# The triangular substitution of a hybrid encoder block's time mixer, on VectorE instead of GpSimd

## The chip, the cores and the metric

The kernel runs on one core of a Trainium2 chip. The metric is the device time of one execution in microseconds (us). Times quoted per run are those of whole executions; times of stages are counted from the first instruction of one profiled execution.

## The reference

The reference is one encoder block on `x` of 256 tokens by 2048 columns, all in float32: a projection, two mixers side by side, an output projection with layer norm, and a SwiGLU feed-forward with layer norm.

```python
proj = jnp.einsum('bsd,dc->bsc', x, w_in[l])
y_fourier = _fourier_mixer(proj[..., F_OFF:R_OFF])        # 512 columns, FFT over tokens and group
y_rwkv = _rwkv7_bidir(proj[..., R_OFF:], ...)             # 24 heads of 64, both directions
mix = jnp.einsum('bsc,cd->bsd', jnp.concatenate([y_fourier, y_rwkv], -1), w_out[l])
h = _layernorm(ALPHA * x + mix, ln1_g[l], ln1_b[l])
ff = jax.nn.silu(h @ w_ffn_gate[l]) * (h @ w_ffn_up[l])
x = _layernorm(ALPHA * h + ff @ w_ffn_down[l], ln2_g[l], ln2_b[l])
```

The bidirectional time mixer carries, for each head and direction, a 64 by 64 state over the tokens:

```python
sa = jnp.einsum('bhij,bhj->bhi', state, a_t)
state = (state * w_t[:, :, None, :] + sa[..., None] * b_t[:, :, None, :]
         + v_t[..., None] * k_t[:, :, None, :])
y_t = jnp.einsum('bhij,bhj->bhi', state, r_t)
```

## The kernel before

The kernel has two parts. The first holds the projection, both mixers, the output projection, the first norm and the start of the feed-forward; the second holds the rest. A float32 weight is split into a rounded part `hi` (ScalarE) and a remainder `lo` (VectorE, or GpSimd for every second half in the projections), and TensorE multiplies with both. `weights` (line 362) loads a block of 512 KB into one of three `raw` buffers and makes two halves in rings of six `hi` and six `lo`.

The time mixer doesn't walk over the tokens one at a time. The 24 heads are 12 pairs, two heads on the 128 partitions, and a loop runs over six double pairs, each with 4 chunks of 64 tokens and both directions. Its steps are:

- `prepare` (line 516), for each pair: projections of `k` and `r` with a token shift, the decays (`e`, `f` by two scans), the normed key `kx`, and the operands `ar` and `xb`. The receptance products are lines 574 to 576: `r` times `f`, once per head, 64 partitions by 512 elements. Masked score products `w` end the step.
- `extract` (line 627), for each pair: the 16 by 16 diagonal blocks of the chunks' triangular matrices go out to DRAM by 16 small copies of SyncE, and come back as one copy into `mt`, one block per partition row.
- `substitute` (line 647), for each double pair: it inverts the 16 by 16 blocks by forward substitution. In step s of 15 a product (into `tmp`) and an addition (into `tt`) take column s of `mt` off the rows below it, for up to 8 columns and both pairs. `tt` then goes to DRAM by one copy of SyncE, comes back into `eb` by 16, and VectorE transposes it into `et`.
- `invert` (line 669): TensorE and small copies build the 64 by 64 inverses `ti` from the blocks.
- `recur` (line 721), for the double pair before: the four chunks in turn (`sv`, `bg`, `v1s`), then the group norm, the bonus and the gate. The result goes to DRAM as `mix`, and later comes back to be split into `xT` for the output projection.

The order in which each engine issues is not written by hand. `Program` collects all operations with what they depend on. `cost` (line 145) gives each an estimate in nanoseconds, `schedule` (line 238) places them with a list scheduler on five engines, and `flush` (line 303) takes the shortest of 49 trial schedules (`TRIES`, line 337) and issues in its order. Operations inside `pr.fused()` are one unit there: their estimates are summed, and nothing of the same engine is issued between them. The estimate for a VectorE operation is line 172:

```python
return 69 + (0.52 if half else 1.04) * n + 60 * ptrs + (110 if part else 0)
```

Before the change the 30 operations of `substitute` are single units on GpSimd, so others of GpSimd can be issued between them.

Of the kernel before, what the change touches and what calls it, by code (L numbers as in the profile page):

```python
# [13 lines left out]
OP = mybir.AluOpType  # L14
# [37 lines left out]
def view(t, off, dims, parts=None):  # L52

    base = t if parts is None else t[parts[0]:parts[1]]
    return bass.AP(tensor=base.tensor, offset=base.offset + off, ap=[list(base.ap[0])] + [list(d) for d in dims])
# [12 lines left out]
class Program:  # L68
# [76 lines left out]
    def cost(self, eng, method, outs, ins, k, args):  # L145
        n = max(self.count(x) for x in outs + ins)
        psum = any("PSUM" in str(x.tensor._space) for x in outs + ins if hasattr(x.tensor, "_space"))
        ptrs = sum(1 for x in ins if self.count(x) == 1) if n > 1 else 0
        kw_op, part = k.get("op"), outs[0].ap[0][1] < 128
        if eng == "pe":  # L150
            n, m = self.count(outs[0]), self.count(ins[0])
            if ins[0].dtype == F32R:
                return max(107, n * 0.455)
            if method == "transpose":
                return 109 if m == 128 and ins[0].ap[0][1] == 128 else 56 if ins[0].ap[0][1] == 128 else 30
            side = 0.5 if ins[0].ap[0][1] == 64 or m == 64 else 1.0
            return max(m, n) * 4 / 2.4 * side + 3 if m != 32 else 15
        if eng == "act":
            return 54 + 0.833 * n + 93 * ptrs + (40 if not psum else 0) + (100 if part and not ptrs else 0)
        if eng == "pool":  # L160
            if kw_op == OP.pow:
                return 1250
            if method == "tensor_tensor":
                return 290 + 2.1 * n
            return (40 if method == "memset" else 147) + (0.9 if method == "memset" else 2.15) * n
        if eng == "sp":
            size = 4 * self.count(outs[0]) * list(outs[0].ap)[0][1]
            return max(330 if size < 16384 else 500, size / 360)
        if method == "reciprocal":
            return 65 + 6.5 * n  # L170
        half = method in ("tensor_copy", "tensor_scalar") and not psum
        return 69 + (0.52 if half else 1.04) * n + 60 * ptrs + (110 if part else 0)
# [6 lines left out]
    def add(self, queue, method, args, kw):  # L179
# [29 lines left out]
        if op < len(self.ops):  # L209
# [3 lines left out]
            o["banks"] |= banks  # L213
            return
        self.ops.append(dict(q=queue, calls=[(method, args, kw)], preds=list(preds), cost=cost, banks=banks,
                             bias=self.bias, rows=ins[0].ap[0][1] / 128 if eng == "pe" else 0,
                             e=["act", "dve", "pool", "pe", "sp"].index(eng), kind=kind))
# [115 lines left out]
EXCL = (1, [[259, 2], [65, 4], [1, 64]])  # L333
# [6 lines left out]
def body(ctx, tc, i, out):  # L340
    nc = tc.nc
    pr = Program(nc)
    act, dve, pool, pe, sp = pr.act, pr.dve, pr.pool, pr.pe, pr.sp
# [61 lines left out]
    with pr.ahead(AHEAD):  # L405
        for q in range(4):
            for j in range(2):
                n, k = 2 * q + j, slice(4 * q + 2 * j, 4 * q + 2 * j + 2)
# [7 lines left out]
                if j == 0:  # L416
                    parts = []
# [51 lines left out]
    for j, tl in enumerate((T_W, T_A)):  # L469
        t = lora[:, 2 + j, :]  # L470
# [3 lines left out]
    for j, tl in enumerate((T_G0, T_G1)):  # L474
        t = lora[:, j, :]
# [40 lines left out]
    def prepare(p, dec):  # L516
# [16 lines left out]
        e, f = R["e"].next(), R["f"].next()  # L533
# [30 lines left out]
        ar, xb = R["ar"].next(), R["xb"].next()  # L564
# [8 lines left out]
        shifted(T_R + p, r)  # L573
        for h, (a0, a1) in enumerate(HEAD):
            rb = r[a0:a1].rearrange("p (c t) -> p c t", t=64)[:, None].to_broadcast([64, 2, 4, 64])
            dve.tensor_tensor(ar[a0:a1, :, :, 1 + h, :], rb, view(f, *EXCL, parts=(a0, a1)), op=OP.mult)
        pool.tensor_tensor(bs, kd[:, 0, :], kd[:, 1, :], op=OP.add)
        dve.scalar_tensor_tensor(bs, bs, col(V_RK, p), r, op0=OP.mult, op1=OP.mult)

# [67 lines left out]
    def substitute(P, mt):  # L647

        msp = ms[P % 2]
        tt, tmp, e, et = (R[n].next() for n in ("tt", "tmp", "eb", "et"))  # L650
        act.copy(tt, eye2[:, None].to_broadcast([128, 2, 8, 16]))
        for s in range(15):
            m, t = min(8, s + 1), 15 - s
            x = tmp[:, 0:2 * m * t].rearrange("p (n j t) -> p n j t", n=2, t=t)
            pool.tensor_tensor(x, mt[:, :, None, s + 1:16, s].to_broadcast([128, 2, m, t]),
                               tt[:, :, 0:m, s:s + 1].to_broadcast([128, 2, m, t]), op=OP.mult)
            pool.tensor_tensor(tt[:, :, 0:m, s + 1:16], tt[:, :, 0:m, s + 1:16], x, op=OP.add)
        with pr.ahead(AHEAD):
            sp.dma_start(out=msp.rearrange("(n p) x -> p n x", n=2), in_=tt.rearrange("p n m t -> p n (m t)"))
            for j in range(2):  # L660
                for n, (h, b, a) in enumerate(quads):
                    for k in range(2):
                        r = a + 16 * k
                        sp.dma_start(out=e[r:r + 16, 8 * j:8 * j + 8, 16 * k:16 * k + 16],
                                     in_=msp[j * 128 + r:j * 128 + r + 16].rearrange("(c u) (m t) -> (u m) c t", u=2, t=16))
        dve.transpose(et.rearrange("p c t -> p (c t)"), e.rearrange("p c t -> p (c t)"))
        return (e, et), (et, e)
# [184 lines left out]
    for P in range(NPAIR // 2 + 1):  # L852
        if P < NPAIR // 2:
            dec, mt = R["dec"].next(), R["mt"].next()
            sts = []
            for n in range(2):
                sts.append(prepare(2 * P + n, dec[:, n]))
                if P == 1 and n == 0:
                    fourier_in()
                extract(2 * P + n, sts[n], mt)  # L860
                tokens(sts[n])
                sts[n]["v"] = R["v"].next()
                shifted(T_V + 2 * P + n, sts[n]["v"])
            diag = substitute(P, mt)
        if P:
            recur(P - 1, *last)
        if P < NPAIR // 2:
            sv = R["sv"].next()
            for n in range(2):
                values(2 * P + n, sts[n], sv)  # L870
            last = sts, invert(sts, diag), sv, dec
# [49 lines left out]
    for n, k in enumerate(2 * kp + j for kp in ORDER for j in range(2)):  # L921
        m = loads[n % 3]
# [96 lines left out]
    for f in range(FT):  # L1019
# [3 lines left out]
        parts = []  # L1023
# [102 lines left out]
```

## Time and profile before

| | |
|---|---|
| median of 3 runs | 1441.82 us (1440.95 to 1443.12) |
| profiled execution | 1441.34 us |
| its span, first to last instruction | 1439.5 us |
| mean granted TensorE clock, share of full | 0.968 |
| TensorE matmul busy | 1344.1 us, 93% of the span |
| VectorE busy | 852.4 us, 59% |
| ScalarE busy | 704.3 us, 49% |
| GpSimd busy | 398.2 us, 28% |

In the trace PE is TensorE, DVE is VectorE, ACT is ScalarE, POOL is GpSimd and SP is SyncE, whose DMA queue is SPq. Every operation goes through one helper, so all carry its line, 316; they are told apart by the names of what they write and read (`out<-in`, buffer numbers left out). The banks `nar` and `ch` share one name, `ch`. A time in square brackets is how long the engine stood idle before an instruction, with what released it. The mixer and the output projection take about the first 640 us of the span, the feed-forward the rest.

### The profile page before, as it was taken

What the parts mean: (1) busy time and instruction counts of PE and PEld (TensorE: products, weight loads), DVE (VectorE), ACT (ScalarE), POOL (GpSimd) and SP (SyncE); (2) the same over time, 40 slices, a digit from 0 to 9 for tenths busy, and PEclk for the clock granted to TensorE, in tenths of its full rate; (3) what the DMA queues carried; (4) which work ended last, traced back from release to release, by engine and by line L of the source; (5) the groups of instructions that cost most, each with busy time, mean ns of one, the idle gap of its engine ahead of it and who ended that gap; (6) DMA issues with size and microseconds to landing.
All of it is one profiled execution on the core that took longest, in us unless ns stands there. A gap on an engine that the chain in (4) does not pass through costs nothing.

```text
span 1439.5 us, 30790 instructions
## 1 busy us (share of the span) xinstructions
PE 1344.1 (93%) x12132; PEld 1172.2 (81%) x12132; DVE 852.4 (59%) x1427; ACT 704.3 (49%) x1367; POOL 398.2 (28%) x540
## 2 busy tenths in 40 slices
PE   6889899898979888989999999999999999999996
PEld 6888778887878776667888888888888888888896
DVE  4665367576655655556655555555555555555556
ACT  5545445445454543434555555555555554444442
POOL 3548437484744714002211111111111110000002
PEclk9999899899999989999999999999999999999999
DMA  7444423323242346443575555555555555555553
GB/s 243 134 131 133 149 87 113 85 87 99 76 150 74 105 131 192 139 160 131 176 238 187 190 190 184 186 188 190 190 184 186 187 191 190 190 191 192 191 187 132
DMA packets 102696, 228.77 MB, mean 159 GB/s; under 512 B 37528, under 2 KB 48280, under 8 KB 101912
## 3 DMA queue, kind: packets, MB, share of 16 engines
q1 hardware_dynamic: 102552, 226.82, 48.1%
q8 instruction: 95, 1.56, 0.4%
q14 instruction: 49, 0.40, 0.1%
HBM read 220.47 MB, written 6.29 MB: 158 GB/s over the span
## 4 chain that ended last, share of the span: by engine, by line
PE 51%; DVE 0%; DVEq 0%; issue 0%
PE ch L316 19%; PE mm L316 14%; PE sc L316 12%; PE yb L316 6%; DVE w L316 0%; DVE lrs L316 0%; DVEq L1122 0%; DVE lst L316 0%; DVE lmv L316 0%
## 5 line engine op out<-in xcount | busy, mean ns | idle before, releaser
L316 DVE TENSOR_TENSOR lo<-raw,hi 128x512 fp32r<-128x512 f32 x676 | 495.3, 737 | 382.7 <-ACT hi L316 358.5
L316 ACT CAST hi<-raw 128x512 fp32r<-128x512 f32 x760 | 465.7, 620 | 477.6 <-PE mm L316 123.7
L316 PE MATMUL mm<-xT,hi 128*128 128x256 f32 (+1 forms) x1776 | 414.4, 320 | 13.3 <-ACT hi L316 6.4
L316 PEld LDWEIGHTS mm<-xT,hi 128*128 128x128 f32 x1776 | 300.3, 199 | 35.3 <-issue 7.7
L316 PE MATMUL mm<-xT,lo 128*128 128x256 f32 (+1 forms) x1072 | 305.9, 293 | 2.6 <-DVE lo L316 1.7
L316 PEld LDWEIGHTS mm<-xT,lo 128*128 128x128 f32 x1072 | 210.7, 198 | 9.9 <-DVE lo L316 3.4
L316 PE MATMUL ch<-xT,hi 128*128 128x512 f32 x528 | 185.2, 397 | 0.0
L316 POOL TENSOR_TENSOR lo<-raw,hi 128x512 fp32r<-128x512 f32 x84 | 115.0, 1372 | 143.9 <-ACT hi L316 106.9
L316 POOL TENSOR_TENSOR fe<-fe,fe 128x256 f32<-128x256 f32 x44 | 32.7, 745 | 405.7 <-DVE fe L316 385.0
L316 PE MATMUL ch<-xT,lo 128*128 128x256 f32 x528 | 142.6, 281 | 0.0
L316 PE MATMUL sc<-xT,hi 128*128 128x512 f32 x352 | 121.9, 397 | 0.0
L316 PEld LDWEIGHTS ch<-xT,hi 128*128 128x128 f32 x528 | 96.9, 188 | 19.9
L316 PEld LDWEIGHTS ch<-xT,lo 128*128 128x128 f32 x528 | 99.6, 189 | 4.4
L316 PE MATMUL sc<-xT,lo 128*128 128x256 f32 x352 | 93.3, 280 | 0.0
L316 PE MATMUL ch<-hi,h 128*128 128x512 f32 x264 | 88.7, 390 | 0.0
L316 POOL TENSOR_TENSOR lrs<-lrs,mhalf 128x1 f32<-128x1 f32 x4 | 3.9, 972 | 290.5 <-DVE lrs L316 290.5
L316 PEld LDWEIGHTS sc<-xT,hi 128*128 128x128 f32 x352 | 63.9, 188 | 13.1
L316 PE MATMUL mm<-hi,h 128*128 128x512 f32 (+1 forms) x248 | 73.5, 359 | 0.0
L316 PEld LDWEIGHTS sc<-xT,lo 128*128 128x128 f32 x352 | 66.4, 189 | 2.9
L316 PE MATMUL yb<-xT,hi 128*128 128x512 f32 x176 | 63.7, 396 | 0.0
L316 PEld LDWEIGHTS ch<-hi,h 128*128 128x128 f32 x264 | 49.6, 188 | 10.7
L316 POOL TENSOR_TENSOR tmp<-mt,tt 128x96 f32<-128x96 f32 (+13 forms) x90 | 49.2, 547 | 19.2 <-DMA mt<-md 15.4
(214 smaller groups left out, 2058.5 us busy)
## 6 DMA issues: line engine op xcount, KB each, us to landing
raw<-in_w_gu_dram SPq DMA_DIRECT2D x176, 512.0 KB, 3.2
raw<-in_w_down_dram SPq DMA_DIRECT2D x88, 512.0 KB, 3.2
raw<-in_w_in_dram SPq DMA_DIRECT2D x84, 512.0 KB, 3.6
raw<-in_w_out_dram SPq DMA_DIRECT2D x32, 512.0 KB, 3.5
up<-in_lora_up_dram SPq DMA_DIRECT2D x12, 256.0 KB, 5.9
raw<-in_xT_dram SPq DMA_DIRECT2D x8, 256.0 KB, 4.9
raw<-in_w_in_dram SPq DMA_DIRECT2D x8, 256.0 KB
w<-in_x_dram SPq DMA_DIRECT2D x2, 1024.0 KB, 6.5
```

What stands on the lines that cost most here:

```text
L316: getattr(o["q"].engine, method)(*args, **kw)
```

## The change

`substitute` issues its 30 operations on VectorE, inside `pr.fused()`, so that they are one unit of the schedule. The receptance product of the second head of each pair goes to GpSimd; that of the first stays on VectorE. Five estimates of the planner change: a float32 matmul's cost per column, that of a matmul with 32 rows, a GpSimd `tensor_copy` (a formula of its own), the fixed part of a GpSimd `tensor_tensor`, and a small DMA issue of SyncE. Since the schedule is made from the estimates, the order of all engines' instructions in the first part can change, and that of the second as well.

```diff
--- before.py
+++ after.py
@@ -154,18 +154,20 @@
             if method == "transpose":
                 return 109 if m == 128 and ins[0].ap[0][1] == 128 else 56 if ins[0].ap[0][1] == 128 else 30
             side = 0.5 if ins[0].ap[0][1] == 64 or m == 64 else 1.0
-            return max(m, n) * 4 / 2.4 * side + 3 if m != 32 else 15
+            return max(m, n) * 4.5 / 2.4 * side + 3 if m != 32 else 31
         if eng == "act":
             return 54 + 0.833 * n + 93 * ptrs + (40 if not psum else 0) + (100 if part and not ptrs else 0)
         if eng == "pool":
+            if method == "tensor_copy":
+                return 147 + 0.85 * n
             if kw_op == OP.pow:
                 return 1250
             if method == "tensor_tensor":
-                return 290 + 2.1 * n
+                return 160 + 2.1 * n
             return (40 if method == "memset" else 147) + (0.9 if method == "memset" else 2.15) * n
         if eng == "sp":
             size = 4 * self.count(outs[0]) * list(outs[0].ap)[0][1]
-            return max(330 if size < 16384 else 500, size / 360)
+            return max(450 if size < 16384 else 500, size / 360)
         if method == "reciprocal":
             return 65 + 6.5 * n
         half = method in ("tensor_copy", "tensor_scalar") and not psum
@@ -573,7 +575,7 @@
         shifted(T_R + p, r)
         for h, (a0, a1) in enumerate(HEAD):
             rb = r[a0:a1].rearrange("p (c t) -> p c t", t=64)[:, None].to_broadcast([64, 2, 4, 64])
-            dve.tensor_tensor(ar[a0:a1, :, :, 1 + h, :], rb, view(f, *EXCL, parts=(a0, a1)), op=OP.mult)
+            (dve if h == 0 else pool).tensor_tensor(ar[a0:a1, :, :, 1 + h, :], rb, view(f, *EXCL, parts=(a0, a1)), op=OP.mult)
         pool.tensor_tensor(bs, kd[:, 0, :], kd[:, 1, :], op=OP.add)
         dve.scalar_tensor_tensor(bs, bs, col(V_RK, p), r, op0=OP.mult, op1=OP.mult)
 
@@ -649,12 +651,13 @@
         msp = ms[P % 2]
         tt, tmp, e, et = (R[n].next() for n in ("tt", "tmp", "eb", "et"))
         act.copy(tt, eye2[:, None].to_broadcast([128, 2, 8, 16]))
-        for s in range(15):
-            m, t = min(8, s + 1), 15 - s
-            x = tmp[:, 0:2 * m * t].rearrange("p (n j t) -> p n j t", n=2, t=t)
-            pool.tensor_tensor(x, mt[:, :, None, s + 1:16, s].to_broadcast([128, 2, m, t]),
-                               tt[:, :, 0:m, s:s + 1].to_broadcast([128, 2, m, t]), op=OP.mult)
-            pool.tensor_tensor(tt[:, :, 0:m, s + 1:16], tt[:, :, 0:m, s + 1:16], x, op=OP.add)
+        with pr.fused():
+            for s in range(15):
+                m, t = min(8, s + 1), 15 - s
+                x = tmp[:, 0:2 * m * t].rearrange("p (n j t) -> p n j t", n=2, t=t)
+                dve.tensor_tensor(x, mt[:, :, None, s + 1:16, s].to_broadcast([128, 2, m, t]),
+                                  tt[:, :, 0:m, s:s + 1].to_broadcast([128, 2, m, t]), op=OP.mult)
+                dve.tensor_tensor(tt[:, :, 0:m, s + 1:16], tt[:, :, 0:m, s + 1:16], x, op=OP.add)
         with pr.ahead(AHEAD):
             sp.dma_start(out=msp.rearrange("(n p) x -> p n x", n=2), in_=tt.rearrange("p n m t -> p n (m t)"))
             for j in range(2):
```

## Rows read from the trace of the kernel before

**Rows 1.** Page, busy time, share of the span and instructions of each engine

```profile
PE 1344.1 (93%) x12132; PEld 1172.2 (81%) x12132; DVE 852.4 (59%) x1427; ACT 704.3 (49%) x1367; POOL 398.2 (28%) x540
```

**Rows 2.** Busy time (instructions) of PE, PEld, DVE, ACT, POOL; clock; DMA; GB/s

```profile
0.00:640.00 640.00, 560.07 (x7863) 496.10 (x7864) 384.18 (x714) 300.84 (x625) 309.19 (x436) 0.94 0.40 126
```

**Rows 3.** Waits of TensorE, 0 to 640 us: total us, times, longest

```profile
PE ch L316 <- issue: 19.2, 10, 3.5
PE sc L316 <- DVE xb L316: 8.9, 5, 2.6
PE ch L316 <- DVE et L316: 7.3, 3, 4.1
...
PE mm L316 <- ACT xT L316: 5.0, 2, 4.8
...
PE sc L316 <- DVE ar L316: 2.2, 4, 1.0
...
PE mm L316 <- DVE lo L316: 1.3, 3, 0.9
```

**Rows 4.** Timeline of GpSimd, last substitution: start, us, instruction

```profile
535.75 0.25 POOL L316 TENSOR_TENSOR tmp<-mt,tt 128x30 f32<-128x30 f32 x1 [6.54 <-DMA mt<-md]
...
555.97 0.70 POOL L316 TENSOR_TENSOR tt<-tt,tmp 128x16 f32<-128x16 f32 x1
```

**Rows 5.** Timeline of VectorE and TensorE, end of the mixer

```profile
569.33 0.71 DVE L316 STREAM_TRANSPOSE et<-eb 128x512 f32<-128x512 f32 x1 [4.27 <-DMA mix<-yn]
...
625.74 0.80 PE L316 MATMUL mm<-hi,xT 128*128 128x512 f32 x1 [4.80 <-ACT xT L316]
...
626.76 1.05 PE L316 MATMUL mm<-hi,xT 128*128 128x512 f32 x2
...
631.67 0.63 PE L316 MATMUL sc<-hi,xT 128*128 128x512 f32 x2
```

**Rows 6.** Groups of GpSimd by names: count | busy us, mean ns | idle before

```profile
L316 POOL TENSOR_TENSOR tmp<-mt,tt 128x96 f32<-128x96 f32 (+13 forms) x90 | 49.2, 547 | 19.2 <-DMA mt<-md 15.4
L316 POOL TENSOR_TENSOR tt<-tt,tmp 128x96 f32<-128x96 f32 (+13 forms) x90 | 40.6, 451 | 3.5
```

**Rows 7.** Timeline of VectorE, products of two SBUF operands, and a dependent operation

```profile
303.75 0.42 DVE L316 TENSOR_TENSOR r<-pp 128x256 f32<-128x256 f32 x1
304.21 0.48 DVE L316 SCALAR_TENSOR_TENSOR r<-mm,omm,r 128x256 f32<-128x256 f32 x1
...
344.44 0.68 DVE L316 TENSOR_TENSOR ar<-r,f 64x512 f32<-64x512 f32 x1
```

**Rows 8.** Busy time, last substitution to the late xT (columns as in 2)

```profile
535.75:625.74 89.99, 77.16 (x1117) 58.72 (x1116) 46.01 (x122) 36.97 (x80) 24.65 (x40) 0.97 0.52 167
```

**Rows 9.** Timeline of TensorE, the first of its three waits for et

```profile
166.80 0.45 PE L316 MATMUL ch<-et,w 32*32 32x32 f32 x32 [4.14 <-DVE et L316]
```

**Rows 10.** Timeline of VectorE, 455.6 us on, beside the fifth substitution's start

```profile
455.77 0.43 DVE L316 COPY sv<-ch 64x256 f32<-64x256 f32 x1 [2.01 <-ACT sv L316]
457.00 0.42 DVE L316 TENSOR_TENSOR k<-pp 128x256 f32<-128x256 f32 x1 [0.80 <-ACT pp L316]
```

**Rows 11.** Busy time summed over the stretches of the first five substitutions

```profile
sum 175.68, PE 164.84 PEld 148.67 DVE 121.51 ACT 83.53 POOL 152.96; mean PE 32.97 PEld 29.73 DVE 24.30 ACT 16.71 POOL 30.59
```

**Rows 12.** Timelines of GpSimd and VectorE from 46 us

```profile
46.25 1.30 POOL L316 TENSOR_TENSOR lo<-raw,hi 128x512 fp32r<-128x512 f32 x1 [1.33 <-ACT hi L316]
...
46.58 1.25 DVE L316 TENSOR_TENSOR k<-pp 128x256 f32<-128x256 f32 x1 [1.11 <-ACT pp L316]
```

**Rows 13.** Groups by shape: receptance products, and GpSimd's product of 512 elements

```profile
L316 DVE TENSOR_TENSOR ar<-r,f 64x512 f32<-64x512 f32 x24 | 23.6, 984 | 1.7 <-ACT f L316 1.0
...
L316 POOL TENSOR_TENSOR xb<-th,e 128x512 f32<-128x512 f32 x12 | 15.0, 1253 | 0.1
```

**Rows 14.** SyncE's issues into eb (ns min/median/max), and GpSimd's copy of 512

```profile
L316 SPq DMA_DIRECT2D eb<-ms x96: 302/429/1860, 155.8 to 566.0; - x96
...
L316 POOL COPY w<-ar 64x512 f32<-64x512 f32 x12 | 7.1, 613 | 61.9 <-PE ch L316 61.9
```

## The prediction

> **What bounds the kernel now.** I began with the page's busy shares: TensorE is busy for 93% of the span, VectorE for 59%, GpSimd for 28% [rows 1]. The reader is to see that no vector engine is near its limit, so a vector operation matters only through what TensorE waits for. The edited code runs in the mixer, so I then took the stretch of its 640 us: TensorE is busy 560.1 us there, VectorE 384.2, GpSimd 309.2, with a granted clock of 0.94 [rows 2]. TensorE's 79.9 us of idle time there is nearly all that the change can win. The waits of TensorE in that stretch say what it is made of [rows 3]: 19.2 us is time that no engine released, 8.9 us waits for VectorE's `xb`, 7.3 us for its `et` (the transpose behind the substitution), 5.0 us for ScalarE's `xT`, 2.2 us for `ar`, and only 1.3 us for a `lo` half of a weight.
>
> Next I followed one substitution through the timeline. The last one starts on GpSimd at 535.75 us and its last addition ends at 556.67 [rows 4]. Behind it come the copies through DRAM, the transpose at 569.33, the last inversion and recurrence, and then TensorE stands still for 4.80 us, up to 625.74, because the last mixer columns arrive late as `xT`; after the stop its matmuls are spaced at the lower clock level (two take 1.05 us, five us later 0.63) [rows 5]. So at the end of the mixer the chain through the substitution does set the time; before it, TensorE has other products to run.
>
> **The substitution moves.** It is 30 dependent operations, six times. On GpSimd they are busy 49.2 + 40.6 = 89.8 us [rows 6], 15.0 us each time; with other GpSimd work let in between them, the last takes 20.9 us and the other five 32 to 39. VectorE has no such row, so I price it by its rows [rows 7]: a product of 256 elements takes 0.42 us, one of 512 takes 0.68, which is 0.16 us fixed and 1.02 ns an element; a dependent operation starts 0.04 us after the one before it ends. The 15 steps hold 2 x min(8, s+1) x (15-s) elements, 1192 in sum, twice. So 30 x 0.20 + 2384 x 0.00102 = **8.4 us** a substitution, 50 us in all. VectorE would stand at 384 + 50 - 12 (below) = 422 of 640 us, 66%: still no bound. The same 17 SyncE issues follow each substitution as before, and wait for VectorE instead of GpSimd; behind them on SyncE wait weight loads and the next pair's gather.
>
> *At the end of the mixer* the chain gets 20.9 - 8.4 = 12.5 us shorter. TensorE is idle 12.8 us between the start of that substitution and its 4.80 us stop's end [rows 8], and 12 matmuls behind the stop lose some 0.2 us each, 2.4 us. Bounds: nothing (if something else is late next, the last weight loads being nearest) and -12.5. I take the stop and its slow matmuls, **-7.2 us**, as the other idle pieces there belong to the inversion's own steps. What is late next is the inversion, whose buffers the recurrence before it must leave first.
>
> *In the five earlier double pairs* TensorE waited for `et` three times, 7.3 us in sum [rows 3], 4.14 of it the first time [rows 9]. Elsewhere matmuls cover the substitution's 32 to 39 us, and a shorter one is worth nothing. Bounds 0 and -7.3; the transpose waits for 17 issues of SyncE as well as for the substitution, so I take a little over half, **-4 us**.
>
> *The run holds VectorE.* One unbroken run means that what was let in between GpSimd's steps now queues behind 8.4 us: at one such landing these are the recurrence's `sv`, then `k` of the next pair [rows 10], and `lo` halves; ScalarE and TensorE wait for the first, TensorE and SyncE's buffer release for the last. The five stretches in which GpSimd ran them leave VectorE 175.7 - 121.5 = 54.2 us idle [rows 11], more than the 42 us of five runs. Bounds: nothing, if they fill that idle time, and 42 us, if TensorE waits them out. Weight halves are made ahead (1.3 us of waits in 640), which covers the `lo`; if that stock is gone, each run costs up to its length. I take 1 us a run, **+5 us**, near the lower end by the small waits in rows 3.
>
> The low end of the run's own length, 8.4 us, holds only while GpSimd lies still. A VectorE product of 256 elements that began at 46.58, inside GpSimd's split of 46.25 to 47.55, took 1.25 us and not 0.42: it ended 0.28 us after the split did [rows 12]. GpSimd's share without the substitutions is (309.2 - 89.8 + 15) / 640 = 37%, so the run may stretch to 8.4 / 0.63 = 13.3 us. The Trainium skill, "SBUF — State Buffer", section "SBUF: two separate sides", states this as a rule: an operation of VectorE with two SBUF inputs and one of GpSimd that reads SBUF take a shared port pair in turn, each for a whole instruction. The trace agrees, by that 1.25 us. By the row alone I keep 8.4 to 13.3 us as bounds; taken at its full strength, the rule gives the slower rival below, 1449, where the sum here gives 1434.
>
> **The receptance product** of the second head goes to GpSimd, 12 times. On VectorE each takes 0.98 us in the mean [rows 13], 0.68 undisturbed [rows 7]: -12 x 0.98 = -11.8 us of VectorE time. On GpSimd the nearest product of as many elements takes 1.25 us: +15 us. The two heads' products would run in turn by rows 12, so the path to the score matmuls grows by 1.25 - 0.68 = 0.6 us a pair, 7 us if all lay on TensorE's path; it waits 2.2 us for `ar` now. Behind it on GpSimd waits `bs`, which has time. Bounds -2 and +7; **+1 us**.
>
> **The estimates** change only the order in which each engine issues. A 16-row gather or scatter issue takes 0.43 us [rows 14]; the plan says 0.33 now and 0.45 after, and 48 of them per double pair make 4.8 us that SyncE falls behind. A copy of 512 elements on GpSimd takes 0.61 us [rows 14], planned at 1.25 and then 0.58. These two move towards the rows. The plan prices the new VectorE run at 30 x 0.069 + 2384 x 0.00104 = 4.55 us, 3.9 below my price: that moves away. A new order can win at most what TensorE waits on small steps, nearest the 8.9 us for `xb`, or lose as much. I take a quarter, **-2 us**.
>
> The sum is -7.2 - 4 + 5 + 1 - 2 = -7.2 us. The profiled execution took 1441.34 us (span 1439.5 and 1.84 around it), 0.48 under the median of the runs, 1441.82; so **1434.1 us**, said as 1434.
>
> **Rivals.** *Slower: the run is locked apart and TensorE waits.* With GpSimd's splits in turn with its steps a run takes 13.3 us, 8.7 over its plan; whatever VectorE was to make for the recurrence and the next pair comes that much late, and TensorE, which issues in order, stops at the first of them with all products behind it. At 4 us for each of five runs, +20 and not +5: 1434 + 15 = 1449 us. It decides from 2.4 us a run on, where gains of 12.2 are used up. For it: rows 10 and 12, and VectorE is 69% busy in those stretches. Against it: the 54 us of idle time, and few waits for `lo`. It has a chance of 0.27; the Trainium skill's rule named above is this mechanism, and its own part is the lock.
>
> *No difference.* The planner may place the run late, or the last chain's gain may turn into a wait for the inversion or for loads; TensorE's products then take their old time and the terms cancel: 1441 us, chance 0.16. For it: TensorE was busy through most of the substitutions (164.8 of 175.7 us [rows 11]).
>
> *A larger gain.* All 12.5 us of the last chain and all 7.3 us of the waits for `et` go, and the runs hide: 1441.3 - 19.8 = 1421.5 us, chance 0.12. Against it: inversion steps whose waits have no releaser.
>
> **How the numbers follow.** The forecast of 1434 has a chance of 0.45; its own range is 1428 to 1438 (all of the `et` waits and a little more of the last chain, or runs of 2 us). The range of 1421 to 1452 takes in the larger gain and the slower rival with 4.6 us a run. A measurement tells 0.2% (2.9 us) from nothing: faster 0.45 + 0.12 = 0.57, same 0.16, slower 0.27.
>
> **What would show it.** Right: the 30 operations on VectorE in 8 to 10 us, GpSimd near 325 us in all, no 4.80 us stop of TensorE before `xT`, and waits for `et` under 4 us. The lock: VectorE steps of 1 us and more among rows of 0.2 to 0.3, a run of 13 us, and longer waits of TensorE for `sv`, `k`, `xb` or `lo`. The forecast is wrong if the last substitution does not start sooner after its gather, or if the mixer's TensorE idle time grows although its end is free.

## The result and the profile after

The changed kernel takes 1462.01 us in the median of 3 runs (1458.36 to 1464.48), against 1441.82 before: a ratio of 1.0136, 95% interval 1.0100 to 1.0173. It is slower, and outside the forecast range. The profiled execution took 1464.48 us, its span 1462.7.

First the page's busy shares:

```profile
PE 1343.0 (92%) x12132; PEld 1176.9 (80%) x12132; DVE 911.0 (62%) x1595; ACT 704.6 (48%) x1367; POOL 337.4 (23%) x372
```

And the mixer's window (columns as in [rows 2]); what was 640 us long now takes 663:

```profile
0.00:663.00 663.00, 562.06 (x7884) 502.77 (x7885) 444.04 (x886) 302.70 (x628) 247.82 (x268) 0.92 0.40 123
```

Against [rows 2], GpSimd has 61 us less, VectorE 60 us more. TensorE's busy time grew by only 2 us, its idle time from 79.9 to 100.9: the 23 us are idle TensorE time, nearly all. No engine became the bound; VectorE is busy 67% of the mixer.

The waits of TensorE in the stretch (total us, times, longest) say for whom:

```profile
PE ch L318 <- DVE yn L318: 28.4, 5, 7.5
PE ch L318 <- issue: 20.5, 11, 3.2
PE sc L318 <- DVE xb L318: 7.0, 3, 4.4
PE mm L318 <- DVE lo L318: 6.7, 1, 6.7
...
PE ch L318 <- DVE et L318: 0.8, 1, 0.8
PE mm L318 <- ACT xT L318: 0.6, 3, 0.2
```

In [rows 3] `et` stood at 7.3 and `xT` at 5.0: both are nearly gone, as forecast. In their place stands VectorE's `yn`, the group norm's result, which had cost little in the kernel before:

```profile
PE ch L316 <- DVE yn L316: 3.4, 4, 1.0
```

TensorE's timeline has one stop behind each of the six runs:

```profile
129.36 0.58 PE L318 MATMUL mm<-xT,lo 128*128 128x256 f32 x1 [6.70 <-DVE lo L318]
...
223.00 1.11 PE L318 MATMUL ch<-ident,yn 128*128 128x128 f32 x4 [6.97 <-DVE yn L318]
...
309.87 0.47 PE L318 MATMUL ch<-ident,yn 128*128 128x128 f32 x1 [7.39 <-DVE yn L318]
...
398.64 1.12 PE L318 MATMUL ch<-ident,yn 128*128 128x128 f32 x4 [7.47 <-DVE yn L318]
...
485.56 1.11 PE L318 MATMUL ch<-ident,yn 128*128 128x128 f32 x4 [6.40 <-DVE yn L318]
...
574.94 1.98 PE L318 MATMUL sc<-f,ta 128*65 128x129 f32 x8 [4.41 <-DVE xb L318]
```

Together 39.3 us. What stands ahead of the second, first on VectorE's timeline (start, length, instruction):

```profile
209.64 0.69 DVE L318 TENSOR_TENSOR yn<-yb,mv 128x512 f32<-128x512 f32 x1
210.24 1.22 DVE L318 TENSOR_TENSOR k<-pp 128x256 f32<-128x256 f32 x1
211.38 0.19 DVE L318 TENSOR_TENSOR tmp<-mt,tt 128x30 f32<-128x30 f32 x1
...
212.98 1.35 DVE L318 TENSOR_TENSOR tmp<-mt,tt 128x96 f32<-128x96 f32 x1
214.36 0.26 DVE L318 TENSOR_TENSOR tt<-tt,tmp 128x96 f32<-128x96 f32 x1
...
215.73 1.31 DVE L318 TENSOR_TENSOR tt<-tt,tmp 128x120 f32<-128x120 f32 x1
...
222.17 0.19 DVE L318 TENSOR_TENSOR tt<-tt,tmp 128x16 f32<-128x16 f32 x1
222.26 0.68 DVE L318 TENSOR_TENSOR yn<-yn,rs 128x512 f32<-128x512 f32 x1
```

and beside it on GpSimd's:

```profile
211.12 1.83 POOL L318 TENSOR_TENSOR rs<-rs,mhalf 128x8 f32<-128x8 f32 x1
212.92 1.29 POOL L318 TENSOR_TENSOR lo<-raw,hi 128x512 fp32r<-128x512 f32 x1
...
215.63 1.27 POOL L318 TENSOR_TENSOR lo<-raw,hi 128x512 fp32r<-128x512 f32 x1 [1.43 <-ACT hi L318]
```

The group norm takes the mean off on VectorE, lets GpSimd make `rs` (ready at 212.95) and multiplies by it on VectorE. The run of 211.38 to 222.36 stands between these two steps, so the product waits 9.3 us with its inputs ready. TensorE's transposes of `yn` wait for it, and behind them, in TensorE's order, products that need nothing of it. The fifth run stands in the same gap; the third stands ahead of the whole norm and the fourth ahead of `rs`, with the same effect. The first run delays a `lo` half and the sixth an `xb`. Also to be seen: a step of 96 elements takes 1.35 us where GpSimd's split begins at 212.92, its neighbour 0.26.

What the granted clock does behind the stops shows in slices of 10 us (columns as in [rows 2]):

```profile
210.00:220.00 10.00, 6.03 (x50) 5.45 (x48) 9.31 (x23) 3.87 (x8) 5.47 (x4) 0.91 0.31 103
220.00:230.00 10.00, 7.00 (x35) 6.65 (x35) 8.03 (x22) 3.48 (x8) 4.19 (x4) 0.57 0.39 100
230.00:240.00 10.00, 10.00 (x82) 9.82 (x81) 8.40 (x12) 5.88 (x11) 7.84 (x10) 1.00 0.50 135
```

TensorE stands from 216.03 to 223.00; the slice in which the stop ends has a mean of 0.57, near the lower level (1.2 of 2.4 GHz), and the next is back at full clock. Two further stops look alike: 480 to 490 has 0.55, and 570 to 580 has 0.66. Around the other three the slices have 0.79 to 0.87.

### The profile page after: what moved, and what is told of

It reads as the page before. It is cut to its first block, busy times and chain, and to the rows that moved or that the text cites. A ratio compares the mean times of both kernels' runs of the same rounds, so it can differ in the third digit from the quotient of the medians.

```text
span 1462.7 us, 30811 instructions
## 1 busy us (share of the span) xinstructions
PE 1343.0 (92%) x12132; PEld 1176.9 (80%) x12132; DVE 911.0 (62%) x1595; ACT 704.6 (48%) x1367; POOL 337.4 (23%) x372
## 4 chain that ended last, share of the span: by engine, by line
PE 74%; DVE 12%; issue 5%; DMA 4%; ACT 3%; POOL 1%; SPq 0%; DVEq 0%; ACTq 0%; POOLq 0%
PE ch L318 27%; PE mm L318 25%; PE sc L318 15%; PE yb L318 8%; DVE lo L318 2%; DVE tmp L318 1%; DVE tt L318 1%; DVE f L318 1%; DVE w L318 1%; DMA mt<-md 1%; DMA raw<-in_w_down_dram 1%; DMA raw<-in_xT_dram 1%; ACT hi L318 1%; DMA raw<-in_w_in_dram 1%; DVE sv L318 1%
## 5 line engine op out<-in xcount | busy, mean ns | idle before, releaser
L318 DVE TENSOR_TENSOR lo<-raw,hi 128x512 fp32r<-128x512 f32 x676 | 502.6, 748 | 369.1 <-ACT hi L318 342.1
L318 PE MATMUL mm<-xT,hi 128*128 128x256 f32 (+1 forms) x1776 | 409.9, 322 | 13.4 <-ACT hi L318 6.6
L318 PE MATMUL mm<-xT,lo 128*128 128x256 f32 (+1 forms) x1072 | 296.9, 294 | 6.7 <-DVE lo L318 6.7
L318 PEld LDWEIGHTS sc<-xT,hi 128*128 128x128 f32 x352 | 63.9, 188 | 13.1
L318 PEld LDWEIGHTS ch<-hi,h 128*128 128x128 f32 x264 | 49.6, 188 | 10.6
L318 PEld LDWEIGHTS mm<-hi,h 128*128 128x128 f32 x248 | 46.2, 188 | 8.1
```

What stands on the lines that cost most here:

```text
L318: getattr(o["q"].engine, method)(*args, **kw)
```

## The experiments

Three theories stood at the start. **Theory 1:** the unbroken run stops TensorE, whose order is fixed, and its length counts. **Theory 2:** only the plan's price is wrong (4.55 us for a run of 9 to 11); with a right price the planner fits it in. **Theory 3:** it is the other estimates and the new order, whatever the substitution does. Ratios are to the kernel before on the same chip, with 95% intervals.

**Half of each run.** The changed kernel in its own order on every engine, steps 7 to 14 not issued.

```diff
-            for method, args, kw in o["calls"]:
+            for method, args, kw in o["calls"][:o.get("short")]:
...
+        pr.ops[-1]["short"] = 14
```

> Leaves out steps 7 to 14 of each substitution (16 of its 30 operations); every other instruction stands in the changed kernel's order. Theory 1 (TensorE's six stops of 4.4 to 7.5 us, 39.3 us in sum, are the length of the run): the run falls from 11.0 to about 6.4 us, each stop by about 4.6 us, 27 us in all and the slow clock behind them: 1430 to 1438 us. Theory 3 (the new order as such is at fault, through its other estimates): the stops go but other waits take their place, 1452 us or more.

1429.79 us, ratio 0.9929 (0.9902 to 0.9956): about 30 us less than the changed kernel. The second run takes 6.4 us. Its mixer window:

```profile
0.00:629.00 629.00, 553.27 (x7882) 493.87 (x7883) 423.23 (x790) 301.69 (x627) 248.34 (x268) 0.95 0.42 129
```

and on TensorE's timeline the second stop:

```profile
207.56 0.66 PE L318 MATMUL ch<-ident,yn 128*128 128x128 f32 x4 [2.39 <-DVE yn L318]
```

All of the loss is given back, and more: TensorE is idle 75.7 us instead of 100.9, and busy 8.8 us less with nearly the same number of matmuls, at 0.95 instead of 0.92. The length counts, as theory 1 says. The edit also shortens the chain behind the run; what that is worth by itself is tried further down.

**The plan told the run's length**, behind the fused operations:

```diff
+        pr.ops[-1]["cost"] = 11000
```

> The changed kernel, with the planner told that a run takes 11.0 us and not 4.55. Theory 2 (the run does harm only because the plan prices it too low, so that TensorE is given too little to do meanwhile): TensorE's stops behind the run fall under 2 us each, 1430 to 1442 us. Theory 1 (an unbroken run of 11 us harms wherever it stands): 1452 to 1465 us.

1460.11 us, 1.0133 (1.0100 to 1.0166): no gain. The mixer's window:

```profile
0.00:660.00 660.00, 572.67 (x7876) 508.21 (x7877) 433.46 (x884) 302.78 (x627) 243.22 (x268) 0.91 0.39 122
```

The new order leaves TensorE idle for 87.3 us instead of 100.9, and its stops behind the six runs add up to 23.4 us instead of 39.3. But each is still 2.8 to 6.5 us long, TensorE is busy 10.6 us more, at 0.91, and the first five runs grow to 12 to 13 us. So the price shortens the stops and the time does not follow: theory 2, by which only the price is wrong, falls.

**Not fused:** the 30 operations as single units on VectorE.

```diff
-        with pr.fused():
-            for s in range(15):
+        for s in range(15):
```

> The changed kernel without the fused group: the 30 operations stay on VectorE but others may stand between them. Theory 1 (unbroken): the stops of 6 to 7 us are gone, 1432 to 1444 us. Theory 2 (price): the same 30 operations are still priced 6 us too low, so the waits remain in smaller pieces: 1450 to 1460 us.

1445.9 us, 1.0046 (1.0023 to 1.0069); the longest stop for `yn` is 3.6 us, so the stops of 6 to 7 us are gone, as theory 1 said, though the time lies just above its 1444. Without the binding two thirds of the loss go, but the kernel stays slower than before. The last substitution takes 13.7 us here, and TensorE stops 4.10 us for `xT` again.

**Back on GpSimd**, not fused, with the new estimates and the moved product:

```diff
-                dve.tensor_tensor(tt[:, :, 0:m, s + 1:16], tt[:, :, 0:m, s + 1:16], x, op=OP.add)
+            pool.tensor_tensor(tt[:, :, 0:m, s + 1:16], tt[:, :, 0:m, s + 1:16], x, op=OP.add)
```

> The changed kernel with the substitution back on GpSimd as 30 single units; the new estimates and the receptance product on GpSimd stay. Theory 1 and theory 2: no stop of 4 us and more behind a substitution, 1436 to 1446 us. Theory 3 (estimates and receptance product): 1452 to 1465 us.

1451.94 us, 1.0068 (1.0042 to 1.0094). With no substitution on VectorE half of the loss is there, at the edge of theory 3's range: that theory has a part. Against the version before this one, 30 single units on VectorE, the difference is within the intervals.

**Each part alone**, each a part of the change's own diff put into the kernel before. The five estimates (all of the lines in `cost`):

> The kernel before with the five new estimates alone. The version with estimates and receptance product, and the substitution on GpSimd, stood 0.68% over before. Theory A (the estimates reorder the mixer for the worse): 1447 to 1454 us. Theory B (the receptance product on GpSimd does it): 1437 to 1443 us.

1445.3 us, 1.0054 (1.0033 to 1.0075): a small loss, between the two ranges. The receptance product (the one line in `prepare`):

> The kernel before with the second head's receptance product on GpSimd alone. Theory A (estimates): within 3 us of before. Theory B (the product is late on GpSimd, behind its splits and the substitution, and the score matmuls wait for it): 1447 to 1454 us.

1425.9 us, 0.9921 (0.9897 to 0.9945): faster, by some 12 us, which neither theory said. The fused substitution on VectorE (the lines in `substitute`):

> The kernel before with the unbroken substitution on VectorE alone, old estimates, both receptance products on VectorE. Theory 1 (the run of 9 to 11 us stops TensorE, whatever the estimates): six stops of 4 to 7 us, 1450 to 1465 us. If the run harms only together with the new estimates: 1432 to 1443 us.

1451.9 us, 1.0096 (1.0075 to 1.0117), with six stops of 6.4 to 8.3 us behind runs of 8.9 to 11.9. So the parts don't add: +0.5, -0.8 and +1.0% make +0.7%, the change brings +1.4%.

**A shorter chain without the move.** The order of before, steps 7 to 14 left out on GpSimd.

```diff
+            k0 = len(pr.ops)
...
+            for o in pr.ops[k0:]:
+                o["short"] = 0 if s >= 7 else None
```

> The kernel before, every instruction in its order, but steps 7 to 14 of each substitution are left out on GpSimd. It tells what a shorter chain is worth by itself. By the prediction's first two terms the last chain gets some 9 us shorter, the stop of 4.80 us and its slow matmuls go, and the waits for et (7.3 us) with them: 1428 to 1435 us. If TensorE's fixed order finds other waits behind: 1437 to 1442 us.

1435.92 us, 0.9988 (0.9974 to 1.0003): nothing that can be told. Timelines of GpSimd, SyncE, VectorE and TensorE:

```profile
542.47 0.43 POOL L316 TENSOR_TENSOR tt<-tt,tmp 128x126 f32<-128x126 f32 x1
...
550.19 0.32 SPq L316 DMA_DIRECT2D mix<-up  x1
550.60 0.39 SPq L316 DMA_DIRECT2D ms<-tt  x1
...
562.95 0.71 DVE L316 STREAM_TRANSPOSE et<-eb 128x512 f32<-128x512 f32 x1 [1.70 <-DMA eb<-ms]
...
620.60 0.80 PE L316 MATMUL mm<-hi,xT 128*128 128x512 f32 x1 [4.66 <-ACT xT L316]
```

The last addition ends 13.8 us sooner than in [rows 4], but its copy `ms<-tt` is issued 7.7 us later, behind others in SyncE's order, so `et` comes only 6.4 us sooner than in [rows 5]. The stop of 4.80 is still 4.66 long; it came 5.1 us earlier and did not shrink.

**The order held, the engine changed.** The next kernels take the order that was planned for before, and change only the engine of some operations. First the 30 as one run on VectorE at the place of the first:

```diff
-                getattr(o["q"].engine, method)(*args, **kw)
+                getattr(o.get("on", o["q"]).engine, method)(*args, **kw)
...
+                o["on"], o["first"] = dve, len(pr.ops) - 2 * s - 2
```

> The order of the kernel before on every engine, its own plan; only the 30 operations of each substitution are issued on VectorE, in one run at the place of the first. Theory 1 (the unbroken run itself stops TensorE): six stops of 5 to 9 us, 1455 to 1475 us. If the new plan's order was the cause and not the run: 1436 to 1444 us.

1502.63 us, 1.0436 (1.0397 to 1.0476). The runs take 8.9 to 9.9 us; behind them TensorE stops for 3.5 us once and for 7.7 to 10.4 five times, and it waits for `sv` 47.3 us in all. That is theory 1, with a loss above its range. The fifth, VectorE and TensorE:

```profile
512.00 0.43 DVE L316 COPY sv<-ch 64x256 f32<-64x256 f32 x1
...
512.48 1.01 PE L316 MATMUL ch<-sv,bk 128*64 128x64 f32 x13 [10.10 <-DVE sv L316]
```

That is [rows 10] with a run in front of the copy: TensorE waits it out. The run also makes the last chain shorter, just as predicted: it ends at 601.38, 8.9 us after its start. Yet its copy keeps its place in SyncE's order and is issued 19.1 us later, and the stop before `xT` is as long as in the kernel before (timelines of SyncE and TensorE):

```profile
620.48 0.39 SPq L316 DMA_DIRECT2D ms<-tt  x1
...
689.67 0.80 PE L316 MATMUL mm<-hi,xT 128*128 128x512 f32 x1 [4.81 <-ACT xT L316]
```

The waits for `et` stand at 7.3 us here, as in [rows 3]. Then the 30 on VectorE, but each at its own place, with others in between:

```diff
+            for o in pr.ops[-2:]:
+                o["on"] = dve
```

> The order of the kernel before; the 30 operations are issued on VectorE one by one, each at the place that the plan gave it on GpSimd, with VectorE's other work in between. Theory 1 (unbroken): no stop over 3 us behind it, 1434 to 1446 us. If the 50 us of work more on VectorE are the cost, however broken: 1450 us or more.

1460.31 us, 1.0142 (1.0087 to 1.0196): the longest stop beside a substitution is 4.2 us, for `xb`, which stands at 13.1 in all. The work on VectorE costs here without long stops, as the second expectation says; `et` (6.5) and `xT` (5.1) stay. The product alone, in the old order:

```diff
+            pr.ops[-1]["on"] = (dve, pool)[h]
```

> The order of the kernel before; only the second head's receptance product is issued on GpSimd, at its place. If the 0.8% gain of that part alone came from the engine: 1424 to 1431 us. If it came from the order that the planner made anew: within 3 us of before, or up to 5 us over it by the wait for GpSimd.

1445.29 us, 1.0037 (1.0017 to 1.0058): no gain from the engine by itself. And in the changed kernel's own order, GpSimd's `lo` halves of the projections replaced by memsets of them, which read no SBUF:

```diff
+            if shared and j:
+                pr.ops[k0]["calls"] = [("memset", (lo.bitcast(F32), 0.0), {})]
```

> The order of the changed kernel; GpSimd writes zeros into its 84 remainders lo of the projections instead of subtracting, which leaves out that part of the products and reads no SBUF. If the shared port stretches the runs, each takes 9.0 us and not 11.0, the stops fall by 2 us each, and VectorE's other operations by their stretches: 1445 to 1452 us. If the stretch has another cause, runs of 11 us and 1458 to 1464 us.

1438.05 us, 0.9979 (0.9960 to 0.9998). The same places as above, on the timelines of VectorE and TensorE:

```profile
200.97 0.33 DVE L318 TENSOR_TENSOR tmp<-mt,tt 128x96 f32<-128x96 f32 x1
...
202.73 0.28 DVE L318 TENSOR_TENSOR tt<-tt,tmp 128x120 f32<-128x120 f32 x1
...
208.18 0.19 DVE L318 TENSOR_TENSOR tt<-tt,tmp 128x16 f32<-128x16 f32 x1
...
209.01 1.11 PE L318 MATMUL ch<-ident,yn 128*128 128x128 f32 x4 [4.47 <-DVE yn L318]
```

and in the waits of TensorE:

```profile
PE ch L318 <- DVE yn L318: 18.5, 5, 4.7
```

The steps of 1.35 and 1.31 us are back at 0.33 and 0.28, the first five runs at 9.0, the six stops fall from 39.3 to 25.0 us. A run of 9.0 that the plan holds for 4.55 stops TensorE 4.47. The whole gain of some 23 us is more than these 14: a memset takes 0.53 us instead of 1.27 and frees other VectorE operations too, so the lock's price in the stops is 14 us at most.

**Which part of an order pays.** The order of the product's kernel (`ar_only`), the product back on VectorE:

```diff
+            pr.ops[-1]["on"] = dve
```

> The order of the version with the receptance product alone on GpSimd (ar_only, 0.79% under before), but that product is issued on VectorE at its place. If that gain is the order's: 1424 to 1431 us again. If it is the engine's: 1436 us or more.

1436.53 us, 0.9969 (0.9946 to 0.9993): 0.3% comes with the order, the other 0.5% with the engine in that order. The product on GpSimd and 30 single units on VectorE, old estimates (the edits of `ar_only` and `unfused` together):

> Old estimates; receptance product on GpSimd, the substitution's 30 operations on VectorE as single units. If VectorE is a good place for an unbroken-free substitution, as 1445.9 against 1451.9 with the new estimates says (-0.4%): 1418 to 1428 us. If the planner's new order decides: anywhere from 1425 to 1450.

1455.86 us, 1.0106 (1.0078 to 1.0134), above both ranges; TensorE's waits for `lo` stand at 10.4 us. The same with five fused runs of three steps, priced as measured:

```diff
+        for g in range(0, 15, 3):
+            with pr.fused():
...
+            pr.ops[-1]["cost"] = sum(400 + 4.08 * min(8, s + 1) * (15 - s) for s in range(g, g + 3))
```

> Old estimates; receptance product on GpSimd; the substitution on VectorE as five runs of three steps, each of 1.1 to 2.2 us and priced as measured (0.20 us an operation and 1.02 ns an element). Theory 1: a stop is the run less what TensorE has ready, so runs of 2 us stop nothing: no stop over 3 us behind it, 1420 to 1435 us. If any VectorE substitution costs its 50 us of work: 1445 us or more.

1443.8 us, 1.0024 (0.9999 to 1.0049): no difference from before, and above theory 1's range. One stop is long against its expectation, 5.98 us for `yn`, whose steps on VectorE stand between the short runs of the last substitution. The change with 30 single units, each priced as measured:

```diff
+            for o in pr.ops[-2:]:
+                o["cost"] = 200 + 1.02 * 2 * m * t
```

> The changed kernel with 30 single units on VectorE, each priced as measured (0.20 us and 1.02 ns an element). Against the same with the too low price (1445.9 us): if the price is what is left of the loss, 1430 to 1442 us; if not, within 4 us of 1446.

1446.29 us, 1.0044 (1.0025 to 1.0063), as without the price. No kernel with the whole substitution on VectorE and the rest of the work done was faster than the one before.

**Again, in five rounds,** the fastest version and the change:

> The kernel before with the second head's receptance product on GpSimd alone, again, in five rounds. If the gain is the version's own: 0.986 to 0.996 of before. If it was that chip's or that hour's: within 0.3% of before.

1428.8 us, 0.9919 (0.9902 to 0.9936). The product alone beats both kernels.

> The changed kernel beside it on the same chip: 1.010 to 1.018 of before, as first measured.

1460.91 us, 1.0140 (1.0120 to 1.0160).

## Why the prediction was wrong, step by step

**The end of the mixer, -7.2: the stop went, the gain did not come.** From the start of the last substitution to the first matmul behind `xT` took 89.99 us before [rows 8]. In the changed kernel it takes 81.7, and the stop of 4.80 is gone (timelines of SyncE and TensorE):

```profile
574.11 0.38 SPq L318 DMA_DIRECT2D ms<-tt  x1
...
646.77 0.73 PE L318 MATMUL mm<-hi,xT 128*128 128x512 f32 x2 [0.22 <-ACT xT L318]
```

But TensorE has less to do in that stretch. Here are the stretch ahead of the last substitution in the kernel before, and the two stretches of the changed kernel (columns as in [rows 2]):

```profile
0.00:535.75 535.75, 468.64 (x6697) 425.84 (x6697) 328.84 (x578) 258.83 (x536) 284.54 (x397) 0.94 0.38 120
...
0.00:565.11 565.11, 475.55 (x6861) 435.32 (x6862) 384.96 (x743) 261.77 (x543) 242.81 (x262) 0.92 0.38 117
565.11:646.77 81.66, 70.29 (x954) 54.01 (x952) 46.04 (x122) 33.09 (x72) 5.02 (x6) 0.92 0.47 154
```

The last stretch has 954 matmuls instead of 1117, and TensorE's idle time in it fell only from 12.8 to 11.4 us: a new stop of 4.41 stands there, behind the sixth run. Ahead of it the idle time grew from 67.1 to 89.6 us. So some 22 of the span's 23.2 us were lost in the stretch in which I had priced +5.

The mechanism failed as well in the order of before. With a chain shorter by 13.8 us on GpSimd the stop stayed at 4.66 us, and with the run on VectorE at 4.81; in both the copy `ms<-tt` kept its place in SyncE's order, 7.7 and 19.1 us behind the end of the chain. In the changed kernel the copy is issued at 574.11, right behind the run's end at 574.09. So the term leans on SyncE's order, which I had named and not costed. What the shorter chain alone did in the new order is not shown.

**The waits for `et`, -4: the number came, the reason is not shown.** They fell from 7.3 to 0.8 us, nearer the far bound. But in the order of before they stayed at 6.6 us with the shorter chain on GpSimd and at 7.3 with the run on VectorE. The fall came with the new order.

**The run holds VectorE, +5 at 1 us a run: this step failed.** The first five stops are 34.9 us, 7.0 a run, and the slower clock behind some of them is on top. The first of them, 6.70 us, was for a `lo` half, which I had taken as covered by halves made ahead. I named `sv`, `k` and `lo` as what queues behind a run, and then let 54 us of VectorE idle time and the small waits of [rows 3] argue for the low end. Both are true and neither bears on it. Idle time somewhere in a stretch does not help an operation that stands right behind the run in VectorE's order, and waits are small in an order in which nothing held VectorE that long. The row that did bear on it was [rows 10], `sv` and `k` beside a substitution; with a run ahead of it, it gave 10.10 us. The wait that came in the changed kernel, for `yn`, I had not named: its two VectorE steps lie around a GpSimd step, and the planner put the second and the fifth run into that gap and the third and fourth ahead of it. The upper bound of 42 us held for the stops.

**The run's length, 8.4 us undisturbed: 8.98** where GpSimd lies still (565.11 to 574.09), 9.0 in all of the first five runs where memsets stand for its splits, 10.9 to 11.3 in the five real ones; the bounds 8.4 to 13.3 held. The lock of [rows 12] was rightly read. The Trainium skill, "SBUF — State Buffer", section "SBUF: two separate sides", states that the shared port pair goes for the whole instruction to whichever starts first, a VectorE operation with two SBUF inputs or a GpSimd operation that reads SBUF. The splits and the memsets agree with it: single steps took 1.31 and 1.35 us beside a split of 1.27 to 1.29 us, and none did beside a memset. Beside `rs` no step was held: that operation reads SBUF too and ran on GpSimd from 211.12 to 212.95, and the steps from 211.38 on took 0.19 to 0.30 us. So a span on GpSimd does not by itself tell how long VectorE is held.

**The slower rival** named the mechanism: a run over its plan, VectorE's next product late, TensorE stopped with all behind it. Its 4 us a run was too little by 3. With GpSimd's splits out of the way the stops are still 25.0 us, so the run's own length is the larger part and the lock the smaller. In the one order of the changed kernel, at the second place, runs of 11.0, 9.0 and 6.4 us stopped TensorE for 6.97, 4.47 and 2.39: the length less some 4.0 to 4.5 us. That is near the 4.55 that the plan held for it; that the price makes this room is argued, not shown.

**The product, +1:** as a swap of engines in the old order +0.4%, 5 us, within its bounds of -2 and 7; with the order that comes with it, -0.8%, some 12 us, outside them. Each took 1.62 us on GpSimd, where I had 1.25. **The estimates, -2:** alone +0.5%. I had taken a new order to be a small gain because two prices moved towards the rows. Why one order is better than another stays open: the product alone on GpSimd gave 1.0037 in the old order and 0.9921 in a new one, the same operations on the same engines, and the runs do not show which placement does it. Open too is how the order with the right price lost with its clock what it won in its waits.

## What to carry to other kernels

Before a chain moves to a faster engine, look at what that engine feeds next in program order: TensorE's next product came through VectorE, and an unbroken run there stopped it in the changed kernel for the run's length less some 4 us, and in the order of before, which held no room for it, for about its whole length at most places, however idle VectorE was on average. Look too at what hands the chain's result on: a shorter chain won nothing while its copy kept its place in SyncE's order. An engine that lies idle and feeds nobody in a hurry, as GpSimd here, can be the better place for a chain of small steps, though it takes longer there: with the old estimates and the product on GpSimd it gave 0.9921, and VectorE 1.0024 and 1.0106. With the new estimates the two places could not be told apart. To judge a move in a planned kernel, hold the order fixed and change only the engine, and measure each part alone: the parts did not add, and one of them by itself was the better kernel.

## What the hardware showed beyond expectation

A stop of TensorE can be paid again behind it. With half of each run left out, 25.2 us of idle time went and 8.8 us of busy time with it, for nearly the same matmuls; where three stops of 4.4 to 7.0 us ended, the slices had a granted clock of 0.55 to 0.66. Stops behind runs are not the only place: the kernel before has such a slice too, among matmuls many of which are 32 by 32. In the order with the run priced at 11 us the waits were shorter and the clock fell further. The first line is of the kernel before, the second of that order:

```profile
170.00:180.00 10.00, 7.83 (x273) 7.15 (x272) 3.69 (x6) 5.06 (x10) 4.73 (x5) 0.50 0.39 133
...
220.00:230.00 10.00, 8.45 (x59) 7.51 (x56) 9.73 (x30) 2.26 (x6) 8.36 (x7) 0.50 0.33 80
```

TensorE counts as busy for 8.45 of the second line's 10 us, at the lower level throughout. No list of waits tells that; it shows in the busy time and in the clock beside it.
